# One half for GpSimd and ScalarE, the other for VectorE, in the last stage of a two-layer decoder trunk

## The chip, the cores and the metric

The kernel runs on one core of one Trainium2 chip. The time is device microseconds of one execution, as the median of several. A core has five engines that run their own instruction streams side by side: TensorE (matrix products, PE in the profile; its weight loads are PEld), VectorE (DVE), ScalarE (ACT), GpSimd (POOL) and SyncE (SP), which here issues all transfers between device memory and SBUF, the on-chip memory. Matmul results go to PSUM.

## The reference

Two layers on 256 tokens of width 1024. Each layer normalises its input, projects it to queries, keys, values and a gate, runs attention with 16 heads of 64, multiplies by the gated signal, projects back and adds to the residual. Then comes one final RMSNorm, and this is what the change is about:

```python
def rmsnorm(x, g):
    xf = x.astype(jnp.float32)
    y = xf * lax.rsqrt(jnp.mean(xf * xf, axis=-1, keepdims=True) + NORM_EPS)
    return (y * g.astype(jnp.float32)).astype(x.dtype)
...
    for i in range(DEPTH):
        hn = rmsnorm(h, norm_g[i])
...
        o = o.reshape(B, S, MIX_WIDTH) * jax.nn.silu(z)
        h = h + o @ w_out[i]
    return rmsnorm(h, final_g)
```

So for each of 256 tokens the kernel needs the sum of squares of 1024 numbers, one number 1/rms from it, and 1024 products of a residual, that number and a gain.

## The kernel before, in words

All matmuls keep 32-bit precision by splitting operands into a high and a low part, so most products are three matmuls (high by high, high by low, low by high). Weights arrive by transfers from device memory during the run, and ScalarE (line 113) and VectorE (line 114) split them. The residual `h` is held with features on partitions, in eight tiles of 128 by 256 tokens. Towards the end of the second layer `to_rows` (lines 447 to 455) turns it, so that tokens lie on the partitions.

The last projection, `outp_r` (lines 457 to 500), is called twice: for the first half of the heads with `final` false, then for the second with `final` true. The final call goes over two blocks of 128 tokens, `t` = 0 and 1. A block of 1024 columns is made in pieces: 512 and 512 columns for `t` = 0, and 512, 384 and 128 columns for `t` = 1 (lines 463 to 465). For each piece TensorE runs twelve matmuls (lines 475 to 477) into a PSUM tile. VectorE adds the tile to the residual (line 479). The sum of squares of the first piece is ScalarE's (line 483), with a small add of epsilon by VectorE (line 484); the later pieces are reduced by VectorE, each starting from the sum so far (line 486). Meanwhile GpSimd multiplies the first quarter of each half by the final gain into `hf` (line 489). When the sum is complete, GpSimd raises it to -0.5 (line 492, the number is called `ms`). Then, for each half, ScalarE scales the quarter in `hf` by `ms` (line 495), VectorE makes the other quarter from residual, `ms` and gain in one instruction (line 496), and SyncE issues the stores (line 500): one store of 256 KB for each half at `t` = 0, two of 128 KB for each half at `t` = 1.

Each engine runs its instructions in one order, which a planner works out beforehand: it goes by the priorities written in the program and by a simulated timeline. Where an instruction waits, those behind it on its engine wait too. SyncE's queue holds the stores in the order of the loop.

Of the kernel before, what the change touches and what calls it, by code (L numbers as in the profile page):

```python
# [9 lines left out]
F32 = mybir.dt.float32  # L10
BF16 = mybir.dt.bfloat16
F32R = mybir.dt.float32r
AF = mybir.ActivationFunctionType
OP = mybir.AluOpType

S, D, H, HD, P = 256, 1024, 16, 64, 128
# [28 lines left out]
def trunk(ctx: ExitStack, tc: tile.TileContext, xT, gf, sinks, consts, masks, wkva, w, out):  # L45
    nc = tc.nc
    const = ctx.enter_context(tc.tile_pool(name="const", bufs=1))
    wp = ctx.enter_context(tc.tile_pool(name="wp", bufs=4))
    act = ctx.enter_context(tc.tile_pool(name="act", bufs=1))
# [3 lines left out]
    @contextmanager  # L53
    def at(p):
        old = tc.cur_priority
        tc.cur_priority = int(p * 1000)
        yield
        tc.cur_priority = old
# [3 lines left out]
    h = hg[:, 2 * KT:].rearrange("p (k s) -> p k s", s=S)  # L62
# [38 lines left out]
    def split(j):  # L101
        pieces = []
        for r in chunks[j][0]:
            n = r.shape[-1]
            w = chunks[j][1]
            if len(los) in NATIVE:
                los.append(None)
                pieces.append([r.rearrange("p (k n) -> p k n", n=w), None])
                continue
            a = wp.tile([P, n], F32R, name="whi", bufs=NHI)  # L110
            b = wp.tile([P, n], F32R, name="wlo", bufs=NLO)
            for c0, c1 in (((0, 256), (256, 512), (512, n)), ((0, 512), (512, n)))[len(los)] if len(los) < 2 else ((0, n),):
                ia = nc.scalar.activation(a[:, c0:c1], r[:, c0:c1], AF.Copy)  # L113
                ib = nc.vector.tensor_sub(b[:, c0:c1], r[:, c0:c1], a[:, c0:c1].bitcast(F32))  # L114
            if PACE and len(los) >= PACE and los[-PACE] is not None:
                tc.add_manual_dep(ia.ins, los[-PACE].ins.name, SYNC, reason="pace")
            los.append(ib)
            pieces.append([x.rearrange("p (k n) -> p k n", n=w) for x in (a, b)])
        return pieces
# [87 lines left out]
    for layer in range(2):  # L207
# [115 lines left out]
        for t in range(T):  # L323
            nc.scalar.activation(vs[:, t], pv[:, t].rearrange("p (n d) -> p n d", d=HD), AF.Copy,
                                 scale=rstd[:, t:t + 1])
# [131 lines left out]
        def outp_r(c, final):  # L457
            with at(B + PRI["so%d" % c]):
                hw = split(jo[c])
            with at(B + PRI["o%d" % c]):  # L460
                for t in range(T):
                    tok = slice(t * P, (t + 1) * P)
                    cols = [(0, 512), (512, 512)]
                    if final and t == 1:
                        cols = [(0, 512), (512, 384), (896, 128)]
                    st = work.tile([P, 4], F32, name="st")
                    if final:
                        hf = act.tile([P, 2, 2, P], F32, name="hf", tag="quad", bufs=6)
                        gk = gfin.rearrange("p (k s) -> p k s", s=P)
                    for j, (c0, n) in enumerate(cols):  # L470
                        ps = psum.tile([P, n], F32, name="mm", bufs=NMM)
                        for k in range(4):
                            wh, wl = (x[:, k % 2, c0 % 512:c0 % 512 + n] for x in hw[c0 // 512 * 2 + k // 2])
                            gh, gl = gt[c, k // 2][:, k % 2, 0, tok], gt[c, k // 2][:, k % 2, 1, tok]
                            nc.tensor.matmul(ps, gh, wh, start=k == 0, stop=False)  # L475
                            nc.tensor.matmul(ps, gh, wl, start=False, stop=False)  # L476
                            nc.tensor.matmul(ps, gl, wh, start=False, stop=k == 3)  # L477
                        hv = h[:, c0 // P:(c0 + n) // P, tok]
                        nc.vector.tensor_add(hv, hv, ps.rearrange("p (k s) -> p k s", s=P))
                        if final:  # L480
                            sq = work.tile([P, 512], F32, name="t2")[:, :n].rearrange("p (k s) -> p k s", s=P)
                            if j == 0:
                                nc.scalar.activation(sq, hv, AF.Square, scale=1.0 / 32.0, accum_out=st[:, :1])
                                nc.vector.tensor_scalar(st[:, :1], st[:, :1], EPS, None, op0=OP.add)
                            else:
                                nc.vector.tensor_tensor_reduce(out=sq, in0=hv, in1=hv, scale=1.0 / D, scalar=st[:, j - 1:j],
                                                               op0=OP.mult, op1=OP.add, accum_out=st[:, j:j + 1])
                            if c0 % 512 == 0:
                                nc.gpsimd.tensor_mul(hf[:, c0 // 512], hv[:, :2], gk[:, c0 // P:c0 // P + 2])
                    if final:  # L490
                        ms = work.tile([P, 2], F32, name="ms")
                        nc.gpsimd.tensor_tensor(ms[:, 1:], st[:, len(cols) - 1:len(cols)], mhalf[:, :1], op=OP.pow)
                        o = act.tile([P, 8, P], F32, name="of", tag="quad", bufs=6)
                        for i in range(2):
                            nc.scalar.activation(o[:, 4 * i:4 * i + 2], hf[:, i], AF.Copy, scale=ms[:, 1:])
                            nc.vector.scalar_tensor_tensor(o[:, 4 * i + 2:4 * i + 4], h[:, 4 * i + 2:4 * i + 4, tok],
                                                           ms[:, 1:], gk[:, 4 * i + 2:4 * i + 4], op0=OP.mult, op1=OP.mult)
                            for j in (range(2) if t else (0,)):
                                k0, k1 = (4 * i + 2 * j, 4 * i + 2 * j + 2) if t else (4 * i, 4 * i + 4)
                                nc.sync.dma_start(out[tok, k0 * P:k1 * P], o[:, k0:k1].rearrange("p k s -> p (k s)"))  # L500

        def attn_c(c, qs):
            for i, (b, u) in enumerate(ORDERS[layer][c]):
# [13 lines left out]
        if layer == 0:  # L517
            outp_t(0, False)
            outp_t(1, True)
        else:  # L520
            to_rows()
            outp_r(0, False)
            outp_r(1, True)
# [66 lines left out]
```

## Time and profile before

| what | value |
|---|---|
| median of 3 runs (range) | 222.79 us (222.77 to 223.54) |
| the profiled execution | 223.15 us |
| span of its trace, first to last instruction | 221.3 us |
| mean granted TensorE clock | 0.989 of full speed |
| TensorE busy | 212.5 us, 96% of the span |
| VectorE busy | 157.6 us, 71% |
| ScalarE busy | 128.7 us, 58% |
| GpSimd busy | 63.5 us, 29% |

The span runs from the first to the last instruction of the trace; what the execution takes beyond it lies around it. A share of busy time is an average over the whole span; what a stage is limited by is read from that stage's own rows. Rows of instructions give the start in us from the span's start, the duration in us, the engine, the line of the kernel and the operation with its output and inputs; a square bracket tells how long the engine was idle before and what ended that.

### The profile page before, as it was taken

How to read it: one execution, taken by the hardware profiler on the slowest of the kernel's cores; microseconds unless marked ns; L12 is line 12 of the kernel's file. 1: busy time of each engine (PE TensorE's matmuls, PEld its weight loads, DVE VectorE, ACT ScalarE, POOL GpSimd, SP SyncE). 2: the span in 40 equal slices, each digit the busy share in tenths (PEclk: the TensorE clock that was granted, in tenths of full speed). 3: DMA queues.
4: the chain of work that ended last, by engine and by line, in shares of the span. 5: the costliest groups of instructions: out<-in, count | busy, mean ns of one | idle time of the engine just before them, and what ended most of it. 6: DMA issues, size and time to landing. Idle time of an engine off the chain costs nothing.

```text
span 221.3 us, 4120 instructions
## 1 busy us (share of the span) xinstructions
PE 212.5 (96%) x1535; PEld 185.9 (84%) x1535; DVE 157.6 (71%) x291; ACT 128.7 (58%) x323; POOL 63.5 (29%) x69
## 2 busy tenths in 40 slices
PE   8989999999999999999999999999999999999970
PEld 4879999986989778989999999999799987668870
DVE  2458767858777769958975586889637799577471
ACT  7593355785469445327971555383967985843121
POOL 2562960220241712013631362320620011011231
PEclk9999999999999999999999999999999999999995
DMA  5899998535152323354534476654410000000022
GB/s 172 280 400 412 405 392 288 167 143 169 44 170 77 115 64 129 95 175 123 172 115 142 156 244 182 186 193 129 114 76 3 1 4 0 0 0 3 0 95 95
DMA packets 10532, 31.71 MB, mean 143 GB/s; under 512 B 1296, under 2 KB 2704, under 8 KB 10512
## 3 DMA queue, kind: packets, MB, share of 16 engines
q1 hardware_dynamic: 10512, 31.45, 42.7%
q8 instruction: 12, 0.20, 0.4%
q14 instruction: 8, 0.07, 0.1%
HBM read 30.39 MB, written 1.05 MB: 142 GB/s over the span
## 4 chain that ended last, share of the span: by engine, by line
PE 88%; ACT 3%; DMA 3%; SPq 2%; DVE 1%; issue 1%; POOL 0%; POOLq 0%; ACTq 0%
PE mm L152 12%; PE mm L151 11%; PE mm L150 11%; PE mm L148 9%; PE sc L349 6%; PE o L392 6%; PE tr L377 5%; PE mm L438 4%; PE mm L439 4%; PE mm L440 3%; PE mm L477 3%; PE mm L475 3%; PE mm L476 3%; DMA hg<-xT 3%; PE sc L353 3%; SPq L95 1%
## 5 line engine op out<-in xcount | busy, mean ns | idle before, releaser
L114 DVE TENSOR_TENSOR wlo<-wraw,whi 128x1024 fp32r<-128x1024 f32 (+2 forms) x48 | 60.2, 1257 | 19.3 <-ACT whi L113 15.0
L113 ACT ACTIVATE whi<-wraw 128x1024 fp32r<-128x1024 f32 (+2 forms) x48 | 48.7, 1025 | 40.2 <-DVE wlo L114 29.9
L150 PE MATMUL mm<-quad,whi 128*128 128x256 f32 x216 | 64.0, 298 | 0.1
L152 PE MATMUL mm<-quad,wlo 128*128 128x256 f32 x216 | 62.0, 289 | 0.1
L151 PE MATMUL mm<-quad,whi 128*128 128x256 f32 x216 | 61.5, 286 | 0.0
L150 PEld LDWEIGHTS mm<-quad,whi 128*128 128x128 f32 x216 | 41.3, 192 | 1.1 <-ACT whi L113 0.6
L151 PEld LDWEIGHTS mm<-quad,whi 128*128 128x128 f32 x216 | 41.4, 191 | 1.0 <-issue 0.4
L152 PEld LDWEIGHTS mm<-quad,wlo 128*128 128x128 f32 x216 | 41.0, 191 | 0.8 <-DVE wlo L114 0.3
L363 ACT ACTIVATE p<-sc,nm 128x128 f32<-128x128 f32 (+1 forms) x64 | 26.0, 425 | 15.9 <-DVE nm L359 9.1
L148 PE MATMUL mm<-xf,wraw 128*128 128x256 f32 x112 | 26.9, 380 | 0.7 <-ACT xf L168 0.7
L148 PEld LDWEIGHTS mm<-xf,wraw 128*128 128x128 f32 x112 | 20.2, 190 | 3.4 <-ACT xf L168 1.1
L423 POOL TENSOR_TENSOR th<-th,z 128x256 f32<-128x256 f32 x9 | 8.7, 967 | 42.8 <-ACT th L421 42.6
L355 DVE TENSOR_REDUCE nm<-sc 128x4 f32<-128x1024 f32 (+1 forms) x12 | 14.6, 1220 | 7.2 <-PE sc L353 7.2
L242 POOL TENSOR_TENSOR t<-t,csr 128x512 f32<-128x512 f32 (+1 forms) x7 | 11.4, 1624 | 26.0 <-DVE t L238 18.9
L405 POOL TENSOR_TENSOR quad<-gf,quad 128x256 fp32r<-128x256 f32 x7 | 5.2, 742 | 46.5 <-ACT quad L404 46.5
L438 PE MATMUL mm<-quad,whi 128*128 128x256 f32 x64 | 18.3, 291 | 0.0
L439 PE MATMUL mm<-quad,whi 128*128 128x256 f32 x64 | 18.2, 285 | 0.0
L440 PE MATMUL mm<-quad,wlo 128*128 128x256 f32 x64 | 18.0, 282 | 0.0
L170 DVE SCALAR_TENSOR_TENSOR quad<-hg,quad 128x256 fp32r<-128x256 f32 x16 | 11.1, 702 | 7.1 <-ACT quad L169 7.1
L349 PE MATMUL sc<-ks,qs 64*128 64x128 f32 (+1 forms) x128 | 15.2, 348 | 0.0
L377 PE MATMUL tr<-cst,p 128*128 128x128 f32 x96 | 14.6, 275 | 0.0
L180 POOL TENSOR_TENSOR sq<-sq 128x256 f32<-128x256 f32 x14 | 11.9, 849 | 6.8 <-ACT sq L177 6.0
(105 smaller groups left out, 387.8 us busy)
## 6 DMA issues: line engine op xcount, KB each, us to landing
wraw<-w SPq DMA_DIRECT2D x50, 512.0 KB, 4.8
wraw<-wkva SPq DMA_DIRECT2D x2, 512.0 KB, 8.6
wraw<-w SPq DMA_DIRECT2D x3, 256.0 KB, 4.2
hg<-xT SPq DMA_DIRECT2D x2, 256.0 KB, 6.4
wraw<-gf SPq DMA_DIRECT2D x1, 512.0 KB, 3.5
out<-of SPq DMA_DIRECT2D x2, 256.0 KB, 2.2
out<-of SPq DMA_DIRECT2D x4, 128.0 KB, 1.9
hg<-xT SPq DMA_DIRECT2D x3, 128.0 KB, 3.5
```

Of the source, the lines that this page charges most:

```text
L113: ia = nc.scalar.activation(a[:, c0:c1], r[:, c0:c1], AF.Copy)
L114: ib = nc.vector.tensor_sub(b[:, c0:c1], r[:, c0:c1], a[:, c0:c1].bitcast(F32))
L148: nc.tensor.matmul(ps, wh, x, start=start, stop=stop)
L150: nc.tensor.matmul(ps, wh, xh, start=start, stop=False)
L151: nc.tensor.matmul(ps, wh, xl, start=False, stop=False)
L152: nc.tensor.matmul(ps, wl, xh, start=False, stop=stop)
L349: nc.tensor.matmul(sc[:, par, i], qs[half, 2 * us[0] + i, b * P:(b + 1) * P], ks[half, (h0 + n) // per, :nk], start=i == 0, stop=False)
L363: nc.scalar.activation(p[:, n], sc[:, n % 2, n // 2], AF.Exp, bias=nm[:, n:n + 1], accum_out=rs[:, n:n + 1])
L377: nc.tensor.transpose(pt[:, n], p[:, n0 + n, kt * P:(kt + 1) * P], ident)
L438: nc.tensor.matmul(ps, wh, gh, start=k == 0, stop=False)
L439: nc.tensor.matmul(ps, wh, gl, start=False, stop=False)
L440: nc.tensor.matmul(ps, wl, gh, start=False, stop=k == 3)
```

## The change

`hf` becomes one tile of 512 columns. GpSimd multiplies the whole first half by the gain, in one instruction behind the first piece, and nothing for the second half. Behind the power, ScalarE scales the first half in one instruction, and VectorE makes the second half in one. Each half leaves in one store of 256 KB, for both blocks of tokens.

```diff
                     if final:
-                        hf = act.tile([P, 2, 2, P], F32, name="hf", tag="quad", bufs=6)
+                        hf = act.tile([P, 4, P], F32, name="hf", tag="quad", bufs=6)
                         gk = gfin.rearrange("p (k s) -> p k s", s=P)
...
-                            if c0 % 512 == 0:
-                                nc.gpsimd.tensor_mul(hf[:, c0 // 512], hv[:, :2], gk[:, c0 // P:c0 // P + 2])
+                            if c0 == 0:
+                                nc.gpsimd.tensor_mul(hf, hv, gk[:, :4])
                     if final:
                         ms = work.tile([P, 2], F32, name="ms")
                         nc.gpsimd.tensor_tensor(ms[:, 1:], st[:, len(cols) - 1:len(cols)], mhalf[:, :1], op=OP.pow)
                         o = act.tile([P, 8, P], F32, name="of", tag="quad", bufs=6)
+                        nc.scalar.activation(o[:, :4], hf, AF.Copy, scale=ms[:, 1:])
+                        nc.vector.scalar_tensor_tensor(o[:, 4:], h[:, 4:, tok], ms[:, 1:], gk[:, 4:], op0=OP.mult, op1=OP.mult)
                         for i in range(2):
-                            nc.scalar.activation(o[:, 4 * i:4 * i + 2], hf[:, i], AF.Copy, scale=ms[:, 1:])
-                            nc.vector.scalar_tensor_tensor(o[:, 4 * i + 2:4 * i + 4], h[:, 4 * i + 2:4 * i + 4, tok],
-                                                           ms[:, 1:], gk[:, 4 * i + 2:4 * i + 4], op0=OP.mult, op1=OP.mult)
-                            for j in (range(2) if t else (0,)):
-                                k0, k1 = (4 * i + 2 * j, 4 * i + 2 * j + 2) if t else (4 * i, 4 * i + 4)
-                                nc.sync.dma_start(out[tok, k0 * P:k1 * P], o[:, k0:k1].rearrange("p k s -> p (k s)"))
+                            nc.sync.dma_start(out[tok, 512 * i:512 * i + 512],
+                                              o[:, 4 * i:4 * i + 4].rearrange("p k s -> p (k s)"))
```

## Rows read from the trace of the kernel before

**Rows 1.** The page's head and its first part: busy time of an engine, share of the span, instructions.

```profile
span 221.3 us, 4120 instructions
...
PE 212.5 (96%) x1535; PEld 185.9 (84%) x1535; DVE 157.6 (71%) x291; ACT 128.7 (58%) x323; POOL 63.5 (29%) x69
```

**Rows 2.** Timeline of TensorE in the last stage: the last matmul of the 512-wide, the 384-wide and the 128-wide piece of the second token block.

```profile
210.65 0.39 PE L477 MATMUL mm<-whi,quad 128*128 128x512 f32 x1
...
212.80 0.33 PE L477 MATMUL mm<-whi,quad 128*128 128x384 f32 x1
...
214.15 0.28 PE L477 MATMUL mm<-whi,quad 128*128 128x128 f32 x1
```

**Rows 3.** Timeline of VectorE from 208 us on. L479 is the add, L486 the reduction of squares, L496 the output (x2: two instructions in one row).

```profile
208.35 0.69 DVE L479 TENSOR_TENSOR hg<-hg,mm 128x512 f32<-128x512 f32 x1 [1.08 <-PE mm L477]
209.07 1.33 DVE L486 CUSTOM_DVE_ANT_1 t<-hg,st 128x512 f32<-128x512 f32 x1
...
211.08 0.88 DVE L496 SCALAR_TENSOR_TENSOR of<-hg,ms,wraw 128x256 f32<-128x256 f32 x2 [0.67 <-POOL ms L492]
211.88 0.68 DVE L479 TENSOR_TENSOR hg<-hg,mm 128x512 f32<-128x512 f32 x1
...
213.48 0.55 DVE L479 TENSOR_TENSOR hg<-hg,mm 128x384 f32<-128x384 f32 x1
214.06 1.19 DVE L486 CUSTOM_DVE_ANT_1 t<-hg,st 128x384 f32<-128x384 f32 x1
...
215.18 0.28 DVE L479 TENSOR_TENSOR hg<-hg,mm 128x128 f32<-128x128 f32 x1
215.49 0.35 DVE L486 CUSTOM_DVE_ANT_0 t<-hg,st 128x128 f32<-128x128 f32 x1
...
216.52 0.88 DVE L496 SCALAR_TENSOR_TENSOR of<-hg,ms,wraw 128x256 f32<-128x256 f32 x2 [0.67 <-POOL ms L492]
```

**Rows 4.** Timeline of GpSimd from 205 us on: L489 is the premultiply, L492 the power.

```profile
206.40 0.74 POOL L489 TENSOR_TENSOR hf<-hg,wraw 128x256 f32<-128x256 f32 x1 [4.79 <-DVE hg L479]
209.12 0.74 POOL L489 TENSOR_TENSOR hf<-hg,wraw 128x256 f32<-128x256 f32 x1 [1.98 <-DVE hg L479]
210.49 0.56 POOL L492 TENSOR_TENSOR ms<-st,mhalf 128x1 f32<-128x1 f32 x1 [0.63 <-DVE st L486]
212.64 0.74 POOL L489 TENSOR_TENSOR hf<-hg,wraw 128x256 f32<-128x256 f32 x1 [1.59 <-DVE hg L479]
214.10 0.73 POOL L489 TENSOR_TENSOR hf<-hg,wraw 128x256 f32<-128x256 f32 x1 [0.72 <-DVE hg L479]
215.93 0.56 POOL L492 TENSOR_TENSOR ms<-st,mhalf 128x1 f32<-128x1 f32 x1 [1.10 <-DVE st L486]
```

**Rows 5.** Timeline of ScalarE, second token block: the square of the first piece and the two scaled quarters.

```profile
212.65 0.63 ACT L483 ACTIVATE t<-hg 128x512 f32<-128x512 f32 x1 [0.66 <-DVE hg L479]
...
216.52 0.91 ACT L495 ACTIVATE of<-hf,ms 128x256 f32<-128x256 f32 x2 [3.15 <-POOL ms L492]
```

**Rows 6.** Timeline of SyncE, narrow windows: issues of stores, the two of the first token block and the first and the last of the four of the second.

```profile
211.63 0.35 SPq L500 DMA_DIRECT2D out<-of  x1
...
212.08 0.37 SPq L500 DMA_DIRECT2D out<-of  x1
...
217.03 0.33 SPq L500 DMA_DIRECT2D out<-of  x1
...
218.43 0.40 SPq L500 DMA_DIRECT2D out<-of  x1
```

**Rows 7.** Transfers, with their size and the us from issue to landing: the first and the second store of the first token block, the last store of the second, and two early loads (median).

```profile
out<-of SPq DMA_DIRECT2D x1, 256.0 KB, 2.0
...
out<-of SPq DMA_DIRECT2D x1, 256.0 KB, 2.3
...
out<-of SPq DMA_DIRECT2D x1, 128.0 KB, 1.9
...
hg<-xT SPq DMA_DIRECT2D x2, 256.0 KB, 6.4
```

**Rows 8.** The last piece of the chain of work that ended last, in order of time.

```profile
217.03 0.40 ACTq L586
```

**Rows 9.** SyncE's list of waits from 216 us on: us in total, times, longest.

```profile
SPq L586 <- DMA out<-of: 1.4, 1, 1.4
```

**Rows 10.** Timeline of VectorE and GpSimd at earlier places: a subtraction of weights with GpSimd idle, one beside a GpSimd multiply, and an add from PSUM beside another GpSimd instruction.

```profile
140.02 1.22 DVE L114 TENSOR_TENSOR wlo<-wraw,whi 128x1024 fp32r<-128x1024 f32 x1 [0.58 <-ACT whi L113]
141.98 1.29 POOL L242 TENSOR_TENSOR t<-t,csr 128x512 f32<-128x512 f32 x1 [7.44 <-DVE t L238]
142.39 1.96 DVE L114 TENSOR_TENSOR wlo<-wraw,whi 128x1024 fp32r<-128x1024 f32 x1
...
198.64 0.76 POOL L405 TENSOR_TENSOR quad<-gf,quad 128x256 fp32r<-128x256 f32 x1 [12.45 <-ACT quad L404]
198.73 0.68 DVE L479 TENSOR_TENSOR hg<-hg,mm 128x512 f32<-128x512 f32 x1
```

**Rows 11.** Groups of instructions by line and shape over the whole span: busy us, mean ns of one.

```profile
L495 ACT ACTIVATE of<-hf,ms 128x256 f32<-128x256 f32 x4 | 1.8, 502 | 7.1 <-POOL ms L492 7.1
L113 ACT ACTIVATE whi<-wraw 128x256 fp32r<-128x256 f32 x2 | 0.7, 399 | 0.0
...
L496 DVE SCALAR_TENSOR_TENSOR of<-hg,ms,wraw 128x256 f32<-128x256 f32 x4 | 1.8, 482 | 1.3 <-POOL ms L492 1.3
```

## The prediction

> **What bounds the kernel now.** I read the page first: TensorE is busy 212.5 us of a span of 221.3 us [rows 1], so nearly everything is set by its matmuls, and what the change can touch is what comes after the last of them. I then took the matmul rows of the last stage: the last 128-wide piece starts at 214.15 and runs 0.28 us, so TensorE is done at 214.43 and the tail is 221.3 - 214.43 = 6.87 us [rows 2]. Next the rows of VectorE: it adds the 384-wide piece at 213.48, reduces its squares from 214.06 for 1.19 us, and only then, at 215.18, adds the 128-wide piece that TensorE had finished at 214.43; the last reduction starts at 215.49 [rows 3]. So for some 0.7 us the tail waits for VectorE, not for TensorE. Then GpSimd's rows: the power that makes 1/rms starts at 215.93 and lasts 0.56 us, and a premultiply (hf) runs from 214.10 for 0.73 us [rows 4], right beside the long reduction. Behind it ScalarE and VectorE make the four quarters from 216.52, in 0.91 and 0.88 us [rows 3, 5]. SyncE issues the first of four transfers at 217.03, when ScalarE's first quarter is ready, and the last only at 218.43, though all quarters lay ready at 216.52 + 0.91 = 217.43 [rows 5, 6]. That last one lands 1.9 us after its issue [rows 7], at 220.33; the span ends 0.97 us later. The chain of waits closes with ScalarE's queue at 217.03 for 0.40 us [rows 8], far before the span's end, so it misses the transfer; SyncE's own list of waits has it, 1.4 us at the end for the landing of out [rows 9]. I take the landing as what ends the kernel.
>
> **Why the reduction is long.** The 512-wide reduction of rows 0 to 127 took 1.33 us with a premultiply of 0.74 us beside it from 209.12, the 384-wide one 1.19 us with one of 0.73 us beside it, the 128-wide one, with GpSimd idle, 0.35 us [rows 3, 4]. A 128-wide add is 0.28 us, a 384-wide one 0.55, a 512-wide one 0.69; with the 0.07 us that separate the first of these from the 128-wide reduction, 384 and 512 columns alone should take 0.62 and 0.76 us, 0.57 less each than they did. The same is seen elsewhere: VectorE's subtraction of weights, with both inputs in SBUF, takes 1.22 us alone and 1.96 us where a GpSimd multiply ran from 141.98 to 143.27 and it started at 142.39; it overlaps 0.88 us and is 0.74 us longer [rows 10]. An add that reads PSUM took its usual 0.68 us at 198.73 beside a GpSimd row of 198.64 [rows 10]. So I read it as: two-input VectorE work on SBUF stands still while GpSimd multiplies, adds from PSUM don't.
>
> The Trainium skill ("SBUF — State Buffer", section "SBUF: two separate sides") says that VectorE with two SBUF inputs and GpSimd hold one port pair exclusively, whichever starts first keeping it for a whole instruction. The rows agree on the exclusion but not on who wins: VectorE's reductions start 0.04 to 0.05 us before the multiplies, and yet these keep their 0.73 to 0.74 us [rows 3, 4]. By the rule's letter the reductions would not have waited and their length would be their own; that is rival B.
>
> **The change, part by part.**
> 1. *Premultiply.* Four 256-wide multiplies (0.73 to 0.74 us each) become two 512-wide ones; a 512-wide GpSimd multiply alone is 1.29 us [rows 4, 10]. Each now starts behind the add of a row block's first half and no second one follows the later adds. For rows 0 to 127 it starts at 206.40 and is over by 207.7, before the 512-wide reduction at 209.07. That reduction ends at about 209.83 in place of 210.41, the power follows at 209.91 (0.08 us behind, as before) and ends at 210.47.
> 2. *Output of rows 0 to 127.* ScalarE's and VectorE's two quarters each become one half. VectorE: 0.48 us for 256 columns, and 0.27 more for 256 more (0.28 to 0.55 in the adds), 0.75 us. ScalarE: 0.50 us, and 0.23 more (a copy of 256 columns takes 0.40, the square of 512 takes 0.63), about 0.73 us [rows 3, 5, 11]. VectorE is done by 210.50 + 0.75 = 211.25; before, its two quarters held it until 211.96 and the next add started at 211.88. TensorE has that half ready at 210.65 + 0.39 = 211.04 [rows 2]. So the add moves to about 211.19, 0.69 earlier. The stores here keep their size of 256 KB and are long finished before the end.
> 3. *Middle of rows 128 to 255.* The add ends at 211.87; the multiply runs to about 213.25; ScalarE's square (0.63 us at 212.65 before [rows 5]) is over by 212.8. The 384-wide add waits for TensorE, 212.80 + 0.33 = 213.13 [rows 2], and runs 213.16 to 213.71 (0.03 behind, as at 208.35 [rows 3]). GpSimd is idle by then, so the reduction takes 0.62 and ends at 214.35. The 128-wide add is now late because of TensorE: 214.43 + 0.03 = 214.46 against 215.18. Everything behind it moves by **0.72 us**. If the shift of point 2 is lost, the add starts at 211.88 as before, the 512-wide multiply runs 212.64 to 213.93, still clear of the reduction at 214.06, and 0.57 is left.
> 4. *Last output.* The power ends at 216.49 - 0.72 = 215.77. ScalarE's half starts at 215.80 and ends at 216.53; VectorE's ends at 216.55. Measured from the power, the first issue is 0.76 us behind it (216.53) in place of 0.54 (217.03): 0.22 worse. But only two follow each other: the second issues 0.45 us later, the distance of 211.63 and 212.08 [rows 6], at 216.98. The last issue stood 1.94 us behind the power and stands at 1.21: 0.73 gained. A second transfer of 256 KB lands in 2.3 us, the first in 2.0, against 1.9 for the last of 128 KB [rows 7]: 0.4 lost. Net **0.33 us**.
>
> The change adds no wait: the first store needs ScalarE's half alone, the second stands behind it on SyncE's queue and finds its data ready.
>
> Sum: landing at 216.98 + 2.3 = 219.28, span 220.25, 1.05 us less. The profiled execution took 223.15 us (1.85 outside the span) and would take 222.10. The median of the runs is 222.79, 0.36 below the profiled one; the same 1.05 off gives 221.74, forecast **221.75 us**.
>
> The unknown prices: the reduction alone, from 0.55 (the add's row) to 1.19 (its own row); I take 0.62, because the weight subtraction shows the same stretch with a known base. The two large transfers at the end, from 1.9 (the small row) to 6.4, the 256 KB loads among the first inputs [rows 7]; I take the pair of rows 0 to 127, same size, same target. Nothing else hides a cost: the longer multiplies lie beside VectorE's wait for TensorE and beside adds from PSUM.
>
> **Rivals.**
> A, the forecast: both terms, 0.9 to 1.2 us, 221.6 to 221.9. Chance 0.68.
> B, the 1.19 us are the reduction's own: its wide form carries a fixed 0.57 us and no wait. For it: the profile gives the wide form another name, and it has no wide row with GpSimd idle. Against: the subtraction's 0.74. Then only the 0.33 stays: 222.45. Chance 0.11.
> C, the order on VectorE changes: the add of rows 128 to 255 goes ahead of the output of rows 0 to 127, and that output, two SBUF inputs, stands behind the new 1.29 us multiply. It starts at 211.72, waits to about 213.05 and ends at 213.6; the 384-wide add goes at 213.65, the reduction at 214.2, the 128-wide add at 214.75: 0.43 + 0.33 = 0.76 gained, 222.03. The planner puts that output first today [rows 3], and the power is earlier, not later. Chance 0.06.
> D, more than forecast: the last 256 KB also land in 2.0 us, as the first of the pair did. 0.30 more, 221.45. The pair's second was slower because it queues behind the first, which stays so. Chance 0.09.
> E, slower: the large last transfer takes longer where two of them end the kernel. From a landing of 2.3 + 1.05 = 3.35 us on it eats all; halfway to the loads' 6.4, at 4.3, the time is 222.79 + 0.95 = 223.74. Against: the pair at 211.63. Chance 0.06, with what a new order of the planner may do earlier.
>
> **How the numbers follow.** No change means within 0.5%, 1.11 us, about what a measurement of this kernel can tell. A's middle of 1.05 lies just inside; a third of A goes beyond. Faster: 0.23 + D's 0.09 + a little = 0.33. Slower: 0.05 of E. Same: 0.62. The range goes from below D to above B, 221.3 to 222.5, leaving out E and noise.
>
> **What would show it.** The reductions of 512 and 384 columns in 0.6 to 0.8 us with no GpSimd row beside them; the 128-wide add at TensorE's end; a power ending some 0.7 us earlier; two issues 0.45 us apart, the second landing in 2.3 us. A wide reduction still at 1.2 us with GpSimd idle kills point 3 and leaves B; a landing over 3.3 us means E.

## The result and the profile after

The changed kernel takes 221.75 us (median of 9 runs, 221.44 to 222.44) against 222.91 us for the kernel before in the same measurement (9 runs, 222.71 to 223.54). The ratio is 0.9943, with a 95% interval of 0.9929 to 0.9958: faster by 0.57%, by 0.42 to 0.71%. The forecast was 221.75 us. The half per cent that was taken as the bound of no change lies inside the interval, so these runs do not say on which side of it the gain falls.

On every engine the order of the instructions is the same in both kernels, but for the lines of the change. The page's head and first part, after:

```profile
span 220.7 us, 4109 instructions
...
PE 213.0 (97%) x1535; PEld 186.7 (85%) x1535; DVE 156.1 (71%) x289; ACT 128.2 (58%) x321; POOL 63.3 (29%) x67
```

The page gives a span to 0.1 us, which is coarse for what follows. Windows that run up to the last instruction give it to 0.01 us, the first line before the change, the second after (start and end, length, busy time of the five engines, granted clock of TensorE as a share of full speed, share and GB/s of the transfers):

```profile
221.00:221.34 0.34, 0.00 (x0) 0.00 (x0) 0.00 (x0) 0.00 (x0) 0.00 (x0) 0.50 0.00 0
...
220.00:220.66 0.66, 0.00 (x0) 0.00 (x0) 0.00 (x0) 0.00 (x0) 0.00 (x0) 0.50 0.00 0
```

The span is only 0.68 us shorter. This profiled execution took 222.44 us, the longest of the nine, and its TensorE finished late, as its last matmul shows (timeline of TensorE, answering to [rows 2]):

```profile
214.66 0.28 PE L477 MATMUL mm<-whi,quad 128*128 128x128 f32 x1
```

It ends at 214.94, before the change at 214.43. Between executions of kernels that are alike up to this point, that end lies anywhere from 214.09 to 215.19, so I compare tails from here on: from TensorE's end to the span's end it was 221.34 - 214.43 = 6.91 us (6.87 with the page's rounded span), and is 220.66 - 214.94 = 5.72. That is 1.19 us less.

Timeline of VectorE after, from 209 us on, answering to [rows 3] (the output is L495 now):

```profile
209.58 0.75 DVE L486 CUSTOM_DVE_ANT_1 t<-hg,st 128x512 f32<-128x512 f32 x1
...
211.01 0.75 DVE L495 SCALAR_TENSOR_TENSOR of<-hg,ms,wraw 128x512 f32<-128x512 f32 x1 [0.67 <-POOL ms L492]
211.68 0.68 DVE L479 TENSOR_TENSOR hg<-hg,mm 128x512 f32<-128x512 f32 x1
...
213.68 0.55 DVE L479 TENSOR_TENSOR hg<-hg,mm 128x384 f32<-128x384 f32 x1 [0.32 <-PE mm L477]
214.27 0.62 DVE L486 CUSTOM_DVE_ANT_1 t<-hg,st 128x384 f32<-128x384 f32 x1
...
214.97 0.29 DVE L479 TENSOR_TENSOR hg<-hg,mm 128x128 f32<-128x128 f32 x1
215.30 0.35 DVE L486 CUSTOM_DVE_ANT_0 t<-hg,st 128x128 f32<-128x128 f32 x1
...
216.33 0.75 DVE L495 SCALAR_TENSOR_TENSOR of<-hg,ms,wraw 128x512 f32<-128x512 f32 x1 [0.67 <-POOL ms L492]
```

The two wide reductions take 0.75 and 0.62 us where they took 1.33 and 1.19. The 384-wide add now has idle time before it, ended by TensorE, and the 128-wide add starts 0.03 us behind TensorE's end instead of 0.75.

Timeline of GpSimd after, answering to [rows 4]:

```profile
212.44 1.30 POOL L489 TENSOR_TENSOR hf<-hg,wraw 128x512 f32<-128x512 f32 x1 [1.46 <-DVE hg L479]
215.74 0.56 POOL L492 TENSOR_TENSOR ms<-st,mhalf 128x1 f32<-128x1 f32 x1 [2.00 <-DVE st L486]
```

The multiply is over at 213.74, before the reduction of 214.27. The power ends at 216.30, 1.36 us behind TensorE's end (2.06 before).

Timeline of ScalarE, then SyncE's two last issues in narrow windows and the us to landing of each, answering to [rows 5 to 7]:

```profile
216.33 0.72 ACT L494 ACTIVATE of<-hf,ms 128x512 f32<-128x512 f32 x1 [3.15 <-POOL ms L492]
...
217.07 0.33 SPq L497 DMA_DIRECT2D out<-of  x1
out<-of SPq DMA_DIRECT2D x1, 256.0 KB, 2.0
...
217.50 0.38 SPq L497 DMA_DIRECT2D out<-of  x1
out<-of SPq DMA_DIRECT2D x1, 256.0 KB, 2.3
```

The stores go 0.77 and 1.20 us behind the power and the last lands at 219.8; from the power to the span's end it is 4.36 us (4.85 before). So the 1.19 us are 0.70 ahead of the power's end and 0.49 behind it.

### The profile page after: what moved, and what is told of

Its sections match the earlier page's. It is cut to its first block, busy times and chain, and to the rows that moved or that the text cites. A ratio compares the mean times of both kernels' runs of the same rounds, so it can differ in the third digit from the quotient of the medians.

```text
span 220.7 us, 4109 instructions
## 1 busy us (share of the span) xinstructions
PE 213.0 (97%) x1535; PEld 186.7 (85%) x1535; DVE 156.1 (71%) x289; ACT 128.2 (58%) x321; POOL 63.3 (29%) x67
## 3 DMA queue, kind: packets, MB, share of 16 engines
HBM read 30.39 MB, written 1.05 MB: 142 GB/s over the span
## 4 chain that ended last, share of the span: by engine, by line
PE 87%; DMA 3%; ACT 2%; DVE 2%; SPq 2%; issue 2%; POOL 1%; POOLq 0%
PE mm L152 12%; PE mm L151 11%; PE mm L150 11%; PE mm L148 9%; PE sc L349 6%; PE o L392 6%; PE tr L377 5%; PE mm L438 4%; PE mm L439 4%; PE mm L440 3%; DMA hg<-xT 3%; PE mm L477 3%; PE sc L353 3%; PE mm L475 2%; PE mm L476 2%
```

## The experiments

Each row gives the time as a ratio to the kernel before, run beside it on the same chip, with its interval; then, from the profile, the us from TensorE's end to the power's end, and from there to the span's end. Their sum is the tail. Span ends are to 0.01 us here, as above.

| kernel | ratio (95%) | to the power's end | from there to the end | tail |
|---|---|---|---|---|
| before | | 2.06 | 4.85 | 6.91 |
| after | 0.9943 (0.9929 to 0.9958) | 1.36 | 4.36 | 5.72 |
| after, run again | 0.9952 (0.9935 to 0.9968) | 1.35 | 4.37 | 5.72 |
| after, once more | 0.9952 (0.9938 to 0.9965) | 1.35 | 4.37 | 5.72 |
| multiplies only | 0.9977 (0.9965 to 0.9990) | 1.35 | 4.84 | 6.19 |
| stores only | 0.9967 (0.9953 to 0.9980) | 2.05 | 4.17 | 6.22 |
| multiply put back | 0.9966 (0.9955 to 0.9976) | 1.93 | 4.36 | 6.29 |
| fill put in | one run, 221.91 us | 1.36 | 4.37 | 5.73 |
| multiply in the first block | one run, 222.26 us | 1.36 | 4.37 | 5.73 |
| two issuing engines | 0.9949 (0.9932 to 0.9966) | 1.35 | 4.46 | 5.81 |
| four wide stores | 1.0029 (1.0016 to 1.0042) | 1.36 | 5.95 | 7.31 |
| two stores, short rows | 0.9976 (0.9963 to 0.9989) | 1.35 | 5.05 | 6.40 |
| half by half | 0.9935 (0.9916 to 0.9954) | 1.36 | 4.15 | 5.51 |
| half by half, again | 0.9941 (0.9928 to 0.9954) | 1.36 | 4.15 | 5.51 |

**The changed kernel again** (no edit), as the measure for its neighbours.

> The changed kernel again, as the measure for the runs beside it. My theory has two terms: about 0.70 us because no GpSimd multiply runs beside the 384-wide reduction, and about 0.4 us because the last store is issued earlier. Expected: 1.0 to 1.2 us faster than the kernel before; last matmul to end of power 1.36 us (2.06 before), end of power to end of span 4.4 us (4.8 before).

The kernel before stood at 222.98 to 223.06 us beside these runs, so a ratio of 0.9952, found here and once more below, is 1.07 us. The three tails of the change agree to 0.01 us.

> The changed kernel once more, beside the version that makes its output half by half: 1.0 to 1.2 us faster than before, end of power to end of span 4.4 us.

**Multiplies only.** The change's `hf`, but quarters and four small stores for the second block:

```diff
-                        nc.scalar.activation(o[:, :4], hf, AF.Copy, scale=ms[:, 1:])
-                        nc.vector.scalar_tensor_tensor(o[:, 4:], h[:, 4:, tok], ms[:, 1:], gk[:, 4:], op0=OP.mult, op1=OP.mult)
                         for i in range(2):
+                            nc.scalar.activation(o[:, 2 * i:2 * i + 2], hf[:, 2 * i:2 * i + 2], AF.Copy, scale=ms[:, 1:])
+                            nc.vector.scalar_tensor_tensor(o[:, 4 + 2 * i:6 + 2 * i], h[:, 4 + 2 * i:6 + 2 * i, tok],
+                                                           ms[:, 1:], gk[:, 4 + 2 * i:6 + 2 * i], op0=OP.mult, op1=OP.mult)
+                            for k0 in ((2 * i, 4 + 2 * i) if t else ()):
+                                nc.sync.dma_start(out[tok, k0 * P:k0 * P + 256], o[:, k0:k0 + 2].rearrange("p k s -> p (k s)"))
+                        for i in (() if t else range(2)):
                             nc.sync.dma_start(out[tok, 512 * i:512 * i + 512],
...
```

> Only the first term: GpSimd multiplies the first half in one instruction, but ScalarE and VectorE still work in quarters and the second token block still leaves in four stores of 128 KB. My theory: 0.70 us faster than before (0.65 to 0.75), the last matmul 1.36 us ahead of the end of the power, and the old 4.8 us behind it. The rival, that the gain is made by the stores and the shorter reduction only uncovers another wait: 0.0 to 0.2 us faster.

Its tail is 0.72 us shorter than before the change; by time it is faster by 0.51 us (0.22 to 0.78). The power's end moved by 0.71, the part behind it is the old one (4.84 for 4.85). The rival's 0.0 to 0.2 does not fit.

**Stores only.** The kernel before, with the two large stores:

```diff
-                            for j in (range(2) if t else (0,)):
-                                k0, k1 = (4 * i + 2 * j, 4 * i + 2 * j + 2) if t else (4 * i, 4 * i + 4)
-                                nc.sync.dma_start(out[tok, k0 * P:k1 * P], o[:, k0:k1].rearrange("p k s -> p (k s)"))
+                            nc.sync.dma_start(out[tok, 512 * i:512 * i + 512],
+                                              o[:, 4 * i:4 * i + 4].rearrange("p k s -> p (k s)"))
```

> Only the stores: the kernel before with two stores of 256 KB for the second token block, multiplies and quarters as before. The first half is ready 0.54 us behind the power, the second 0.94; issues at 0.54 and 0.99, last landing 2.3 us later at 3.29 in place of 1.94 + 1.9 = 3.84. My theory: 0.55 to 0.65 us faster than before, so more than the 0.4 us that this part gives in the change, because quarters let the first store go 0.2 us earlier. The rival, that the tail is worth 0.4 us however the halves are made: 0.4. The wide reductions stay at 1.33 and 1.19 us.

Timelines of VectorE, GpSimd and SyncE:

```profile
213.95 1.18 DVE L486 CUSTOM_DVE_ANT_1 t<-hg,st 128x384 f32<-128x384 f32 x1
...
214.00 0.72 POOL L489 TENSOR_TENSOR hf<-hg,wraw 128x256 f32<-128x256 f32 x1 [0.72 <-DVE hg L479]
215.82 0.56 POOL L492 TENSOR_TENSOR ms<-st,mhalf 128x1 f32<-128x1 f32 x1 [1.10 <-DVE st L486]
...
216.96 0.33 SPq L498 DMA_DIRECT2D out<-of  x1
...
217.39 0.37 SPq L498 DMA_DIRECT2D out<-of  x1
```

The long reduction is there, beside its multiply; the stores go 0.58 and 1.01 us behind the power, and the part behind the power is 4.17 us, 0.68 less than before and a little more than the 0.55 to 0.65 expected. So the stores alone are worth 0.68 us, and the change, with its 0.49, gives 0.19 of that back: ScalarE's half of 0.72 us lets the first store go 0.77 us behind the power, and here, with quarters of some 0.50 us, it goes at 0.58. The multiplies' 0.72 and the stores' 0.69 add up to 1.41 us of tail, more than the change's 1.19. These 0.2 us are read from the traces; the intervals of the times are too wide for them.

**Multiply put back.** The change with a premultiply of a quarter of the second half, into a tile that nothing reads:

```diff
                             if c0 == 0:
                                 nc.gpsimd.tensor_mul(hf, hv, gk[:, :4])
+                            elif c0 == 512:
+                                dm = work.tile([P, 2, P], F32, name="dm")
+                                nc.gpsimd.tensor_mul(dm, hv[:, :2], gk[:, 4:6])
```

> The change with one thing put back: GpSimd multiplies the first quarter of the second half by the gain, into a tile that nothing reads, so that it runs beside the wide reductions again. My theory: reductions of 1.33 and 1.19 us again, the 128-wide add 0.6 us later, 0.6 us slower than the change (0.4 to 0.7). The rival, that the reductions became short for another reason (their start, the order, what runs behind them): as the change, and reductions of 0.75 and 0.62 us.

Timelines of VectorE and GpSimd:

```profile
209.15 1.33 DVE L486 CUSTOM_DVE_ANT_1 t<-hg,st 128x512 f32<-128x512 f32 x1
...
214.01 1.19 DVE L486 CUSTOM_DVE_ANT_1 t<-hg,st 128x384 f32<-128x384 f32 x1
...
209.19 0.74 POOL L492 TENSOR_TENSOR dm<-hg,wraw 128x256 f32<-128x256 f32 x1 [1.43 <-DVE hg L479]
...
214.05 0.73 POOL L492 TENSOR_TENSOR dm<-hg,wraw 128x256 f32<-128x256 f32 x1 [0.18 <-DVE hg L479]
```

The reductions have their old lengths to the hundredth, from the multiply alone. The tail is 0.57 us longer than the change's (6.29 to 5.72). By time the medians differ by 0.36 us (222.22 to 221.86), and the intervals of the two ratios overlap, so the size is taken from the trace. This multiply reads columns that the reduction reads too; that shared data are not the cause is seen in [rows 10], where a subtraction of weights was held up beside a multiply with which it shares no tile.

**Fill put in.** The same place, but GpSimd writes zeros and reads nothing; the last line of the edit lets it wait for the add, so that it falls beside the reduction:

```diff
-                        nc.vector.tensor_add(hv, hv, ps.rearrange("p (k s) -> p k s", s=P))
+                        ia = nc.vector.tensor_add(hv, hv, ps.rearrange("p (k s) -> p k s", s=P))
...
+                            elif c0 == 512:
+                                dm = work.tile([P, 512], F32, name="dm")
+                                im = nc.gpsimd.memset(dm, 0.0)
+                                tc.add_manual_dep(im.ins, ia.ins.name, SYNC, reason="beside")
```

> The change, with a GpSimd fill of 512 columns (it writes zeros into a tile that nothing reads, and reads nothing) beside each wide reduction. If any GpSimd instruction holds the reductions up: they are longer than 0.75 and 0.62 us by about the fill's length. If what collides are the reads: 0.75 and 0.62 us as in the change.

Timelines of VectorE and GpSimd:

```profile
209.03 0.75 DVE L486 CUSTOM_DVE_ANT_1 t<-hg,st 128x512 f32<-128x512 f32 x1
...
213.72 0.62 DVE L486 CUSTOM_DVE_ANT_1 t<-hg,st 128x384 f32<-128x384 f32 x1
...
209.05 0.53 POOL L492 MEMSET dm<- 128x512 f32 x1 [1.40 <-DVE hg L479]
...
213.75 0.53 POOL L492 MEMSET dm<- 128x512 f32 x1 [0.55 <-DVE hg L479]
```

A fill of 0.53 us lies wholly beside each reduction and costs it nothing.

**Multiply in the first block.** The multiply put back, with `and t == 0` in its condition.

> The change with a premultiply beside the 512-wide reduction of the first token block alone (into a tile that nothing reads). My theory: that reduction takes 1.33 us again, but what follows waits for TensorE anyway, so the 128-wide add of the second block is late by 0.05 to 0.15 us only. The rival, that the whole delay passes through: 0.57 us.

Timelines of VectorE and TensorE:

```profile
209.39 1.33 DVE L486 CUSTOM_DVE_ANT_1 t<-hg,st 128x512 f32<-128x512 f32 x1
...
214.25 0.62 DVE L486 CUSTOM_DVE_ANT_1 t<-hg,st 128x384 f32<-128x384 f32 x1
...
214.79 0.28 DVE L479 TENSOR_TENSOR hg<-hg,mm 128x128 f32<-128x128 f32 x1
...
214.47 0.28 PE L477 MATMUL mm<-whi,quad 128*128 128x128 f32 x1
```

The 128-wide add starts 0.04 us behind TensorE's end (214.75), 0.01 later than in the change; 0.05 to 0.15 later was expected. What the first block's reduction costs is hidden whole, with no idle time left before the 128-wide add; only the second block's counts.

**Two issuing engines.** The first large store of the second block goes out from ScalarE:

```diff
-                            nc.sync.dma_start(out[tok, 512 * i:512 * i + 512],
+                            (nc.scalar if t and i == 0 else nc.sync).dma_start(out[tok, 512 * i:512 * i + 512],
```

> The change, with the first store of the second token block issued by ScalarE and the second by SyncE, so that neither stands behind the other. If the 0.45 us between two issues of SyncE set the end: the second goes at 0.78 us behind the power in place of 1.20, end of power to end of span 4.0 us. My theory, that with only two stores the bytes behind the first issue set it (0.8 us to the first data, 512 KB in 1.4 us): 4.3 to 4.4 us, no faster than the change.

Timelines of ScalarE's and SyncE's issues, and the landings:

```profile
216.36 0.39 ACTq L497 DMA_DIRECT2D out<-of  x1
216.38 0.33 SPq L497 DMA_DIRECT2D out<-of  x1
...
out<-of SPq DMA_DIRECT2D x1, 256.0 KB, 2.5
out<-of ACTq DMA_DIRECT2D x1, 256.0 KB, 2.7
```

Both stores are issued within 0.02 us of each other, 0.4 us ahead of the change's second, and land later after their issue (2.5 and 2.7 for 2.0 and 2.3). Nothing is gained: 4.46 us for 4.36. With two stores the gap between issues is not the limit; the data start some 0.8 us behind the first issue and then need their time. In the change they flow from inside the first of these windows to inside the last, some 1.4 us, at rates as in the middle one:

```profile
217.80:218.00 0.20, 0.00 (x0) 0.00 (x0) 0.00 (x0) 0.00 (x0) 0.00 (x0) 1.00 0.46 174
218.00:218.20 0.20, 0.00 (x0) 0.00 (x0) 0.00 (x0) 0.00 (x0) 0.00 (x0) 1.00 1.01 379
...
219.20:219.40 0.20, 0.00 (x0) 0.00 (x0) 0.00 (x0) 0.00 (x0) 0.00 (x0) 0.50 0.41 144
```

**Four wide stores.** Two stores of 64 tokens for each half of the second block:

```diff
-                            nc.sync.dma_start(out[tok, 512 * i:512 * i + 512],
-                                              o[:, 4 * i:4 * i + 4].rearrange("p k s -> p (k s)"))
+                            for p0, p1 in ((0, 64), (64, 128)) if t else ((0, 128),):
+                                nc.sync.dma_start(out[t * P + p0:t * P + p1, 512 * i:512 * i + 512],
+                                                  o[p0:p1, 4 * i:4 * i + 4].rearrange("p k s -> p (k s)"))
```

> The change, but each half of the second token block leaves in two stores of 64 tokens and 512 columns: four issues again, rows of 2 KB as in the change (1 KB before). If the number of issues is what the change saved: last issue 2.1 us behind the power, end of power to end of span 4.7 to 5.0 us, as before the change or worse. The rival, that longer rows are what it saved: 4.4 us as in the change.

The last issue, and the transfers' windows:

```profile
218.63 0.59 SPq L498 DMA_DIRECT2D out<-of  x1
```

```profile
218.00:219.00 1.00, 0.00 (x0) 0.00 (x0) 0.00 (x0) 0.00 (x0) 0.00 (x0) 0.50 0.93 205
219.00:220.00 1.00, 0.00 (x0) 0.00 (x0) 0.00 (x0) 0.00 (x0) 0.00 (x0) 0.50 0.91 207
```

The 5.95 us behind the power are outside of both expectations, and the kernel is slower than before the change. Stores of 64 tokens have a price of their own: an issue takes up to 0.59 us, and the data flow at 205 to 207 GB/s where whole blocks reach 379 in the change. So this run says nothing on the count of issues.

**Two stores, short rows.** Two stores again, each of the quarters 0 and 2, or 1 and 3, so that a token's row goes in two pieces of 1 KB:

```diff
+                        ov, sv = out[tok].rearrange("p (a j c) -> p a j c", a=2, j=2), o.rearrange("p (a j k) s -> p a j (k s)", a=2, j=2)
                         for i in range(2):
+                            if t:
+                                nc.sync.dma_start(ov[:, :, i], sv[:, :, i])
+                                continue
```

> The change, but the two stores of the second token block carry the first and third quarter, and the second and fourth: two issues of 256 KB as in the change, rows of 1 KB as before it. If the tail's gain in the change is the number of issues alone: end of power to end of span 4.4 us. If the length of the rows counts too: 512 KB at the 270 GB/s of the kernel before in place of 380 GB/s, 0.4 to 0.5 us more, 4.8 us.

The first issue, its landing, and windows of the transfers:

```profile
216.42 0.64 SPq L499 DMA_DIRECT2D out<-of  x1
out<-of SPq DMA_DIRECT2D x1, 256.0 KB, 2.6
```

```profile
217.60:217.80 0.20, 0.00 (x0) 0.00 (x0) 0.00 (x0) 0.00 (x0) 0.00 (x0) 0.88 0.36 123
218.00:219.00 1.00, 0.00 (x0) 0.00 (x0) 0.00 (x0) 0.00 (x0) 0.00 (x0) 0.50 1.03 347
```

The part behind the power is 5.05 us: 0.68 more than in the change run beside it, with the same number of stores and bytes, so the form of the rows counts beside the number of issues. Here it counts in two ways, an issue of 0.64 us for 0.33 to 0.38, and 347 GB/s for 379. The first is the larger: the data begin some 2.2 us behind the power, for 1.6 in the change. Of that, 0.08 us is not the rows' doing: the first store needs VectorE's half too, and goes 0.85 us behind the power for 0.77.

How much of the kernel before's 4.85 came from its short rows and how much from its four issues is seen in its own trace, in windows of 0.2 us:

```profile
218.00:218.20 0.20, 0.00 (x0) 0.00 (x0) 0.00 (x0) 0.00 (x0) 0.00 (x0) 0.50 1.06 358
218.20:218.40 0.20, 0.00 (x0) 0.00 (x0) 0.00 (x0) 0.00 (x0) 0.00 (x0) 0.50 0.53 164
218.40:218.60 0.20, 0.00 (x0) 0.00 (x0) 0.00 (x0) 0.00 (x0) 0.00 (x0) 0.50 1.04 353
```

Its rows of 1 KB flow at some 350 GB/s, as here, and between two stores the flow dips; the 270 GB/s of the expectation is a mean with the dips in it. An estimate from these rates: 128 KB at 350 GB/s need 0.37 us, less than the 0.43 to 0.49 us between two issues, so each store is all but through before the next begins. The 512 KB would need 1.5 us at 350 GB/s and 1.4 at 379, and took about 1.9 (217.9 to 219.8). So of the half microsecond by which they flow longer than in the change, most is pauses between the issues, and 0.1 us is the short rows.

**Half by half.** From the experiment with the stores alone: the first store should go as early as a quarter allows, and the multiply should stay clear of the reduction. VectorE scales a quarter of the premultiplied half, then makes the other half:

```diff
-                        nc.scalar.activation(o[:, :4], hf, AF.Copy, scale=ms[:, 1:])
-                        nc.vector.scalar_tensor_tensor(o[:, 4:], h[:, 4:, tok], ms[:, 1:], gk[:, 4:], op0=OP.mult, op1=OP.mult)
                         for i in range(2):
+                            if i == 0:
+                                nc.scalar.activation(o[:, :2], hf[:, :2], AF.Copy, scale=ms[:, 1:])
+                                nc.vector.tensor_scalar(o[:, 2:4], hf[:, 2:], ms[:, 1:], None, op0=OP.mult)
+                            else:
+                                nc.vector.scalar_tensor_tensor(o[:, 4:], h[:, 4:, tok], ms[:, 1:], gk[:, 4:], op0=OP.mult, op1=OP.mult)
```

> The change with its output made half by half: ScalarE scales the first quarter, VectorE the second from the premultiplied tile (one SBUF input), then VectorE makes the whole second half. The first store can go 0.54 us behind the power (0.72 to 0.75 in the change), the second at about 1.05 (1.20). My theory, that the tail is set by when the stores start: end of power to end of span 4.15 us as with quarters and two stores, against 4.4 in the change, so 0.2 us faster than the change and 1.3 us faster than before. The rival, that the landing of the two stores is the same bound whatever their start: as the change.

Timelines of VectorE and SyncE:

```profile
215.48 0.35 DVE L497 TENSOR_SCALAR of<-hf,ms 128x256 f32<-128x256 f32 x1 [0.67 <-POOL ms L492]
215.75 0.74 DVE L499 SCALAR_TENSOR_TENSOR of<-hg,ms,wraw 128x512 f32<-128x512 f32 x1
...
216.02 0.33 SPq L500 DMA_DIRECT2D out<-of  x1
...
216.52 0.33 SPq L500 DMA_DIRECT2D out<-of  x1
```

The power ended at 215.45; the stores go 0.57 and 1.07 us behind it, and the span ends 4.15 us behind it, as expected, and as with quarters and two stores (4.17). It was run again beside the change:

> The output made half by half, once more, to measure it beside the change: 1.3 to 1.4 us faster than before, 0.25 us faster than the change; end of power to end of span 4.15 us.

Again it is 4.15 us, with a tail of 5.51 for the change's 5.72 beside it. Medians of 221.51 and 221.48 us lie under the change's 221.86 and 221.72. That it beats the kernel before is sure (0.9941, 0.9928 to 0.9954); that it beats the change, by some 0.2 us, is shown by the traces, while the intervals of the ratios overlap.

## Why the prediction was right

**The bound.** TensorE's end and then a tail that waits, first for VectorE, at the last for the landing: both held. Every gain of these runs is one of the tail.

**The long reduction.** Right, and shown: 0.75 and 0.62 us alone, as worked out from the adds and the 128-wide reduction; 1.33 and 1.19 again when one multiply was put back. Rival B, a fixed price of the wide form, fell with the first trace after, where the form with the same name takes 0.62.

The Trainium skill ("SBUF — State Buffer", section "SBUF: two separate sides") says that VectorE work with two SBUF inputs is held up only by a GpSimd instruction that reads SBUF. The fill, which reads nothing and costs the reduction nothing (0.62 us beside 0.53), agrees. It also says that whichever starts first keeps the port. Here the recorded starts speak otherwise: the reduction's is 0.04 us ahead (214.01 to 214.05 with the multiply put back), the multiply keeps its 0.73 us, and the reduction waits. The measurement decides for this pair; whether the port is asked for later than an instruction is recorded as started, no run here shows.

**Point 1.** Right: the multiply took 1.30 us (1.29 foreseen) and was over 0.53 us before the reduction.

**Point 2.** The shift came (the add started 0.14 us behind TensorE's end of that piece, 211.54, for 0.84 before), but it was not needed. The fallback of point 3, that without it only 0.57 us would be left, is the step that failed: with the first block's reduction long again, the 128-wide add still followed TensorE by 0.04 us. The fallback kept the old start of the add at 211.88 and missed that the first block's output, one instruction of 0.75 us for two of together 0.88, gives 0.13 us back by itself.

**Point 3.** Right: 0.72 us foreseen, 2.06 - 1.36 = 0.70 measured.

**Point 4.** The right direction, but too small: 0.33 foreseen, 4.85 - 4.36 = 0.49 measured. Issues at 0.77 and 1.20 us behind the power (0.76 and 1.21 foreseen) and landings of 2.0 and 2.3 us came as taken from the pair of the first block. From the last landing to the end it was 1.0 us (220.33 to 221.34) and is 0.9 (219.8 to 220.66); the forecast kept 0.97 for both. The multiplies alone, with four small stores, have 1.0 us there, the stores alone 0.9; why is not shown. The rest lies in landings that are known to 0.1 us. The reason given, issues at a fixed distance, holds for the four small stores, whose data pause between them, and is too narrow for two large ones: an estimated 0.69 us for 256 KB at 379 GB/s is longer than the 0.43 us between the issues, and two stores issued at once gained nothing. There the last landing depends on when the first store starts and on how many bytes, in which rows, follow.

**The sum.** 1.05 us were foreseen; the tails give 1.19, the medians 1.16. That the median meets the forecast to the hundredth is luck: the kernel before stood at 222.91 us and not at the 222.79 that the forecast started from, and the gain was larger by about as much.

**Rivals C, D, E.** VectorE's order stayed (C); the second store landed in 2.3 us, not in 2.0 (D), and not in over 3.3 (E).

**The chances.** The likeliest case was put just inside half a per cent; the measured 0.57% lies just outside, by less than its interval. The forecast stood 0.06 us inside that bound, and point 4 alone was off by 0.16, so the split of the chances there rested on less than the sum could carry.

## What to carry to other kernels

A VectorE instruction with two SBUF inputs that is longer than its number of elements says is a reason to look at GpSimd's rows beside it: moving the GpSimd work to a stretch where VectorE waits, or reads PSUM, cost nothing here (in [rows 10] an add from PSUM kept its 0.68 us beside a GpSimd instruction). In a tail that ends with stores, count when the first can go, and make the first store's data first, rather than splitting the work evenly between the engines; and look in narrow windows whether the data pause between the stores. A change with two parts should be tried in parts: here one part gave back 0.2 us of what the other, alone, had gained.

## What was not expected

Stores of 64 tokens flow at little over half the rate of stores of 128 (205 for 379 GB/s) and take up to 0.59 us to issue, for 0.33 to 0.38. A store whose rows go in two pieces of 1 KB takes 0.64 us to issue. And the end of TensorE's work varies by about 1.1 us between executions (214.09 to 215.19), as much as the whole gain, while the tail behind it repeats within 0.01 us in the three runs of the change.
